# The last head pair's first patterns at the end of the far stretch, four projection chunks beside them, and V laid out and loaded by pairs of heads

## The chip, the cores and the metric

The kernel runs on one core of a Trainium2 chip: TensorE (PE) multiplies matrices, VectorE (DVE), ScalarE (ACT) and GpSimd (POOL) do the rest, and SyncE (SP) issues most DMAs. A core has 16 DMA engines. Each engine works through its own instructions in order, and an engine's DMAs stand in that same order: one that waits holds up what is behind it. The metric is the device time of one execution in microseconds, as the median over runs.

## The reference, cut to what matters

One layer of a hybrid encoder on x of 2048 tokens by 1024 features, in float32:

```python
y = rmsnorm(x, g) @ w_in
q, k, v = ...                     # 8 heads of 64; partial rotary on q and k
att = dilated_sliding_attention(q, k, v)
conv = conformer_conv(a, gate, ...)               # depthwise, 31 taps, layernorm, silu
h = x + concat([att, conv]) @ w_out
h = h + cross_attention(rmsnorm(h), rmsnorm(mem)) # 256 memory rows, 4 heads
h = h + square(relu(rmsnorm(h) @ w_up)) @ w_down  # 4096 wide
out = rmsnorm(h, g_final)

for window, d in ((128, 1), (512, 4), (2048, 16)):   # dilated_sliding_attention
    half = window // (2 * d)                         # tokens d apart, 64 to each side
    o, lse = banded_attention(strided(q, d), strided(k, d), strided(v, d), half)
o = sum(softmax(lses) * outs)                        # over the three patterns
```

So each head's attention has three patterns: the first (neighbours), the second (every 4th token) and the third (every 16th), and the three results are weighted by their softmax denominators and added.

## The kernel before, in words

Values are kept in two parts, a high part and the rest (`hi`/`lo`, `h`/`l`), and each product of two float32 matrices is three matmuls (`mm3`, lines 198 to 200). Tokens are worked on in four groups of 512 (p = 0 to 3).

*Start (to about 520 us).* Memory rows, x and the input projection. `lin_v` projects V and stores it as rows of `vtok` in DRAM: one row per token, 8 heads of 130 half floats (64 high, two ones, 64 low). Ahead of it `edges` writes 256 zero rows at each end of `vtok`, out of a tile `zrow` that takes a buffer of the tag `raw`, which the weight loads (`raw_k`, `raw_q` ...) use too.

*The far stretch (about 520 to 770 us).* `att(0, p2_)` works on group 0 and, since the third pattern mixes all tokens, on the third pattern of all four groups (`att_far`). It goes head by head through units of work: four far units, two of the second pattern, two of the first. A unit has three stages, one step apart: scores on PE, minimum (L773, DVE) and exponential (L774, ACT); transposes on PE and their split into `ph` and `pl` (L783, L784); the product with V (`opt`, L788 to L790). `att` yields twice per unit, and `weave` mixes these steps with another generator at a given rate: here the rest of the input projection (`rest`, tile `lin`). `pinned` and `after` hold the order on one engine to the order in which the code is traced; everything else a planner orders by a model of the times, and it draws instructions of later code forward where an engine would be idle in that model.

Far results go to DRAM (`oscr[pr][1]`, POOL's queue), so do the second pattern's (`oscr[pr][0]`). After a pair's last unit `then` starts `combine`: it loads both back (tile `ld`), takes the minimum (L904, L905), weights, sums into `cat`, transposes (`catT`, L940) and leaves the pair's rows `cath`, `catl`. For the last pair (`end`) the rows go straight into the tiles that the output projection reads, and DVE does what POOL does otherwise (`W`).

`load_v` fills three tiles for a pair of heads: `v3` for the far pattern (one DMA), `v2` for the second (eight) and `v1` for the first (five). Each has one buffer, so a load can start when the last product with the previous pair's V is done. In the far stretch all fourteen are issued behind a pair's last unit; in the later groups a pattern's loads are issued behind that pattern.

*After (from about 735 us).* `post(p)` does the output projection, cross attention and MLP of a group; beside it run attention (`att(p + 1)`) and convolution (`conv`, tile `cacc`) of the next. `resid_linear` does the output projection in chunks of 128 features, eight blocks (k) each, of which k = 2 and 3 in the order's last two places are the third and fourth head pair. For group 0 it starts with three chunks at once, so that four k, then two, then two are done for each:

```python
for ms in ((0, 1, 2), (3,), (4,), (5,), (6,), (7,)):
    for ks in (korder[0:4], korder[4:6], korder[6:8]) if len(ms) > 1 else (korder,):
```

The first six of these steps run beside the last steps of group 0's attention (`first`):

```python
weave(islice(pinned(main, "pe"), 6), (first, 2.4))
drain(first)
```

Weights come by `wpost`: a load into `raw` (two buffers), a cast on ACT (L189) and a subtraction on DVE (L190) into `whi` and `wlo`, two buffers in one pool (`wp`) and two in another (`wq`); `wq` takes memory that the far stretch's pool had, whose keys the last units still read. PSUM has eight banks; `banks` names which of them scores (`S`), transposes (`T`), products (`O`) and projections (`mm`) use in turn.

Of the kernel before, what the change touches and what calls it, by code (L numbers as in the profile page):

```python
# [12 lines left out]
F16 = mybir.dt.float16  # L13
# [34 lines left out]
def hybrid_layer(ctx, tc, A, out):  # L48
# [61 lines left out]
    vtok = dr.tile([256 + S + 256, VR], F16, name="vtok")  # L110
# [434 lines left out]
    def lin_v(g, ns):  # L545
# [18 lines left out]
        for t in range(4 * ns[0], 4 * ns[-1] + 4):  # L564
# [10 lines left out]
            s2 = st.rearrange("p h e -> p (h e)")  # L575
            gs = slice(g * 4 * VW, (g + 1) * 4 * VW)
            dma(vtok[256 + P * t:256 + P * (t + 1), gs], s2)
# [259 lines left out]
    def att_far(p2_, h, k, vt, q):  # L837
# [5 lines left out]
        def unit(rq, qh, ql):  # L843
# [40 lines left out]
    def combine(p, pr, o0):  # L884

        if p:
            yield
# [12 lines left out]
        end = p == 0 and pr == H // 2 - 1  # L900
# [6 lines left out]
        for i in range(2):  # L907
            W.tensor_tensor(e3[:, 1 + i], mm_, ld[:, i, :, :, HD + 1], op=ALU.subtract)
# [6 lines left out]
        for i in range(2):  # L915
            W.tensor_tensor(d3[:, 1 + i], e3[:, 1 + i], ld[:, i, :, :, HD], op=ALU.mult)
# [8 lines left out]
        for i in range(3):  # L925
            W.tensor_tensor(e3[:, i], e3[:, i], d2, op=ALU.mult)
        at = aq.tile([P, 4, 2, HD], F32, tag="cat", name=f"cat{p}{pr}")
        for i in range(3):
            src = ld[:, i - 1, :, :, 0:HD] if i else o0[:, :, :, 0:HD]
            W.tensor_tensor(src if i else at, src, e3[:, i].unsqueeze(3).to_broadcast([P, 4, 2, HD]), op=ALU.mult)  # L930
            if i:
                W.tensor_tensor(at, at, src, op=ALU.add)
# [15 lines left out]
    def att_units(p, far, then):  # L948
# [8 lines left out]
        def load_v(pr, pats):  # L957
            es = slice(pr * 2 * VW, (pr + 1) * 2 * VW)
            if 2 in pats and far:
                vt[2] = far.tile([P, 16, 2 * VW], F16, tag="v3", name=f"v3_{pr}")  # L960
                dma(vt[2], vtok[256:256 + S, es].rearrange("(i r) e -> i r e", r=16))
            if 0 in pats:
                vt[0] = aq.tile([P, 5, 2 * VW], F16, tag="v1", name=f"v1_{p}{pr}")
                for c in range(5):
                    t0 = 256 + 512 * p + P * c - 64
                    dma(vt[0][:, c], vtok[t0:t0 + P, es].rearrange("(i r) e -> r i e", r=16))
            if 1 in pats:
                vt[1] = aq.tile([P, 4, 2, 2 * VW], F16, tag="v2", name=f"v2_{p}{pr}")
                for c in range(2):
                    src = vtok[512 * (p + c):512 * (p + c) + 512, es].rearrange("(i a b) e -> b a i e", a=4, b=4)  # L970
                    for b in range(4):
                        dma(vt[1][:, b, c], src[b])

        def unit(pr, hh, pat, g, k, q_, opt, o0):
# [28 lines left out]
            for z in range(2):  # L1003
                blk = 2 * g + z
                for c in range(2):
                    vv = vt[1][:, blk, c] if pat else vt[0][:, blk + c]
# [21 lines left out]
        for pr in range(H // 2):  # L1028
            K = [load_keys(2 * pr + hh, p, hh) for hh in range(2)] if far else None
            o0 = aq.tile([P, 4, 2, ROW], F32, tag="o0", name=f"o0_{p}{pr}", bufs=2)  # L1030
            for hh in range(2):
                h = 2 * pr + hh
                if far:
# [3 lines left out]
                    yield from att_far(far, h, k, vt, q3)  # L1037
# [144 lines left out]
    def resid_linear(load, rhs, korder, resid, hs, ssum, key, y, name, steps=False):  # L1182
# [253 lines left out]
```

## Time and profile before

| | |
|---|---|
| runs, median (lowest to highest) | 2902.63 us (2901.68 to 2903.17) |
| profiled execution, its own time | 2896.44 us |
| its span | 2894.6 us |
| granted clock, mean | 0.992 |
| PE busy | 2826.2 us, 98% |
| DVE, ACT, POOL busy | 1860.5, 1167.0, 472.7 us |
| bytes moved, mean rate | 433.73 MB, 150 GB/s |
| V loads | 208 of 65 KB and 4 of 1040 KB |

The page gives busy time by engine, the chain of work that ended last and the costliest groups; other views give the same for a stretch, a list of who waited for whom, and the instructions in order of time. A line L57 is the helper that issues every DMA. PE's busy time counts a matmul as busy while it is in the pipeline, so rows of matmuls overlap; what counts is the idle time in brackets ahead of an instruction, with what ended it. A wait for several things is put down to the one that came last by the profile.

### The profile page before, as it was taken

To read this page: it belongs to the slowest core of one execution; us is meant where nothing else is said; L and a number is where in the kernel's file an instruction comes from. 1 tells how busy PE (TensorE), PEld (TensorE's weight loads), DVE (VectorE), ACT (ScalarE), POOL (GpSimd) and SP (SyncE) were. 2 spreads that over 40 slices of the span, in tenths; PEclk is the share of its full clock that TensorE was granted. 3 is DMA by queue.
4 is the path that set the end of the run, shared out by engine and by line. 5 is a ranking of instruction groups with operands and counts; after the bars stand their busy time and mean duration, and the time that the engine had idled before them with its cause. 6 is when DMAs were issued, how large, how long until landed. Compare 5 with 4: busy or idle time off the path is not lost.

```text
span 2894.6 us, 41429 instructions
## 1 busy us (share of the span) xinstructions
PE 2826.2 (98%) x15628; PEld 2377.7 (82%) x15628; DVE 1860.5 (64%) x3311; ACT 1167.0 (40%) x1988; POOL 472.7 (16%) x522
## 2 busy tenths in 40 slices
PE   8989999989899999999999999999999999999999
PEld 7878899878788888888888888888888888888888
DVE  5636536455689876566887756689877555544445
ACT  5623211466444343434543344445333433432233
POOL 1336431133002011200022012002111200000000
PEclk9999999999999999999999999999999999999999
DMA  8979854799834444545444546534543445233332
GB/s 259 295 157 228 200 146 134 178 232 237 219 98 127 142 132 126 170 145 164 124 124 128 146 116 192 175 100 121 143 127 115 139 131 175 90 93 100 97 95 73
DMA packets 606656, 433.73 MB, mean 150 GB/s; under 512 B 174886, under 2 KB 537434, under 8 KB 606457
## 3 DMA queue, kind: packets, MB, share of 16 engines
q1 hardware_dynamic: 566904, 408.81, 49.4%
q10 hardware_dynamic: 37952, 16.88, 2.3%
q0 software_dynamic: 1600, 5.41, 0.7%
q8 instruction: 123, 2.02, 0.3%
q14 instruction: 77, 0.62, 0.1%
HBM read 339.89 MB, written 91.11 MB: 149 GB/s over the span
## 4 chain that ended last, share of the span: by engine, by line
PE 84%; DVE 7%; DMA 4%; issue 2%; ACT 1%; SPq 1%; POOL 0%; POOLq 0%; DVEq 0%; ACTq 0%
PE dn L198 8%; PE dn L199 8%; PE dn L200 8%; PE up L198 8%; PE up L200 7%; PE up L199 7%; PE lin L198 4%; PE lin L200 3%; PE lin L199 3%; PE xs L198 2%; PE xs L200 2%; PE xs L199 2%; PE o L198 2%; PE o L199 2%; PE o L200 2%
## 5 line engine op out<-in xcount | busy, mean ns | idle before, releaser
L199 PE MATMUL dn<-hhl,whi_d 128*128 128x512 f32 (+1 forms) x1056 | 403.0, 384 | 1.4 <-DVE hhl L1310 1.4
L198 PE MATMUL up<-mh,whi_u 128*128 128x512 f32 x1024 | 402.6, 393 | 0.5 <-DVE rl L1307 0.5
L198 PE MATMUL dn<-hhh,whi_d 128*128 128x512 f32 (+1 forms) x1056 | 401.5, 391 | 1.1 <-ACT hhh L1309 1.1
L200 PE MATMUL dn<-hhh,wlo_d 128*128 128x512 f32 (+1 forms) x1056 | 402.1, 384 | 0.0
L199 PE MATMUL up<-ml,whi_u 128*128 128x512 f32 x1024 | 399.7, 390 | 1.6 <-DVE ml L1200 1.6
L200 PE MATMUL up<-mh,wlo_u 128*128 128x512 f32 x1024 | 399.8, 391 | 0.0
L215 DVE SCALAR_TENSOR_TENSOR cacc<-cu,cw,cacc 128x512 f32<-128x512 f32 x480 | 387.9, 808 | 5.5
L189 ACT CAST whi_d<-raw_d 128x1024 fp32r<-128x1024 f32 x128 | 134.6, 1052 | 424.8 <-PE up L199 380.0
L1325 DVE TENSOR_TENSOR h<-h,dn 128x512 f32<-128x512 f32 (+1 forms) x264 | 172.1, 666 | 161.8 <-PE dn L200 160.5
L189 ACT CAST whi_u<-raw_u 128x1024 fp32r<-128x1024 f32 x128 | 134.4, 1050 | 327.7 <-PE dn L199 299.6
L1307 DVE SCALAR_TENSOR_TENSOR rl<-up,ssumx 128x512 f32<-128x512 f32 x128 | 87.9, 690 | 260.6 <-PE up L200 256.4
L198 PEld LDWEIGHTS dn<-hhh,whi_d 128*128 128x128 f32 x1056 | 197.8, 188 | 40.7 <-DVE h L1325 3.5
L200 PEld LDWEIGHTS dn<-hhh,wlo_d 128*128 128x128 f32 x1056 | 198.4, 188 | 39.4
L199 PEld LDWEIGHTS dn<-hhl,whi_d 128*128 128x128 f32 x1056 | 198.8, 188 | 37.6 <-DVE hhl L1310 2.3
L199 PEld LDWEIGHTS up<-ml,whi_u 128*128 128x128 f32 x1024 | 192.5, 188 | 40.8 <-DVE ml L1200 3.0
L200 PEld LDWEIGHTS up<-mh,wlo_u 128*128 128x128 f32 x1024 | 192.3, 188 | 40.1
L198 PEld LDWEIGHTS up<-mh,whi_u 128*128 128x128 f32 x1024 | 192.4, 188 | 38.6 <-DVE rl L1307 0.9
L774 ACT ACTIVATE sm<-sm,o 128x256 f32<-128x256 f32 (+1 forms) x384 | 160.1, 465 | 121.8 <-DVE o L773 121.5
L190 DVE TENSOR_TENSOR wlo_u<-raw_u,whi_u 128x1024 fp32r<-128x1024 f32 x128 | 161.6, 1262 | 26.7 <-ACT whi_u L189 26.5
L190 DVE TENSOR_TENSOR wlo_d<-raw_d,whi_d 128x1024 fp32r<-128x1024 f32 x128 | 161.2, 1260 | 23.5 <-ACT whi_d L189 23.4
L773 DVE CUSTOM_DVE_ANT_0 sm<-s,mask 128x256 f32<-128x256 f32 (+1 forms) x384 | 128.3, 374 | 61.2 <-PE s L993 33.8
L176 POOL TENSOR_TENSOR nr<-st_v,mhalf 128x4 f32<-128x4 f32 (+1 forms) x13 | 13.4, 1031 | 845.7 <-DVE st_v L172 845.7
(402 smaller groups left out, 6341.1 us busy)
## 6 DMA issues: line engine op xcount, KB each, us to landing
raw_u<-in_w_up_dram SPq DMA_DIRECT2D x128, 512.0 KB
raw_d<-in_w_down_dram SPq DMA_DIRECT2D x128, 512.0 KB
raw_o<-in_w_out_dram SPq DMA_DIRECT2D x32, 512.0 KB
raw_a<-ascr SPq DMA_DIRECT2D x32, 512.0 KB
raw_b<-bscr SPq DMA_DIRECT2D x32, 512.0 KB
v<-vtok SPq DMA_DIRECT2D x208, 65.0 KB
k<-kscr SPq DMA_DIRECT2D x24, 512.0 KB
k<-kscr SPq DMA_DIRECT2D x8, 1152.0 KB
```

Of the source, the lines that this page charges most:

```text
L176: POOL.tensor_tensor(dst, v, mhalf.to_broadcast([P, v.shape[1]]), op=ALU.pow)
L189: ACT.copy(hi, raw)
L190: (lo_eng or DVE).tensor_tensor(lo, raw, f(hi), op=ALU.subtract)
L198: PE.matmul(o, lh, rh, start=first, stop=False)
L199: PE.matmul(o, lh, rl, start=False, stop=False)
L200: last["pe"] = PE.matmul(o, ll, rh, start=False, stop=end)
L215: DVE.scalar_tensor_tensor(acc, u[:, t:t + 512], cw[:, c, t:t + 1], acc, op0=ALU.mult, op1=ALU.add)
L773: last["dve"] = DVE.tensor_tensor_reduce(dst, so, mask[:, 256 * m:256 * m + nk], 1.0, 3e38, ALU.add, ALU.min, mn)
L774: last["act"] = ACT.activation(dst, dst, AF.Exp, bias=mn, scale=-1.0)
L1307: last["dve"] = DVE.scalar_tensor_tensor(r, pt, 0.0, rsb, op0=ALU.max, op1=ALU.mult)
L1325: last["dve"] = DVE.tensor_tensor(hs[m][:, sl], hs[m][:, sl], pt, op=ALU.add)
```

## The change

- `vtok` is laid out by pairs of heads: four blocks of 2560 rows with 260 half floats each. A V store writes two rows of 520 bytes per token where it wrote one of 1040. The zero rows are written out of 64 partitions in place of 16, still in two DMAs.
- `v3` and `v2` are read in longer runs: `v2` in two DMAs in place of eight (its tile now has the block inside), `v3` still in one, `v1` still in five. For group 1's first pair these loads go by POOL's queue.
- In the far stretch each pattern's V for the next pair is loaded when that pattern is done: `v3` behind the pair's last far unit (`done`), `v2` behind the second pattern, `v1` behind the first.
- For the last pair the first patterns of both heads come at the end, behind both heads' far and second patterns. The second pattern's store goes by SP, and the two loads of the partial sums (`load_sum`) are issued right behind it. For the other pairs of group 0 the minimum of `combine` comes two steps later. Small instructions of `combine` are merged, and one of its three multiplies goes to POOL for the last pair too.
- The output projection of group 0 starts with four chunks (`wide`), in cuts of four, two, one and one k; the fourth chunk has a bank of its own (`m3`, bank 4), and scores have one bank (3) in that time. The steps beside the end of the far stretch go by new rates. The convolution's first eight steps are pinned to PE's order.

```diff
-    vtok = dr.tile([256 + S + 256, VR], F16, name="vtok")
+    vtok = dr.tile([H // 2, 256 + S + 256, 2 * VW], F16, name="vtok")
...
-            dma(vtok[256 + P * t:256 + P * (t + 1), gs], s2)
+            dma(vtok[2 * g:2 * g + 2, 256 + P * t:256 + P * (t + 1)].rearrange("r t e -> t r e"),
+                st.rearrange("p (r h) e -> p r (h e)", r=2))
...
-        zrow = wp.tile([16, 1, VR], F16, tag="raw", name="zrow", bufs=2)
+        zrow = wp.tile([64, 1, VR], F16, tag="raw", name="zrow", bufs=2)
...
-        zb = zrow.to_broadcast([16, 16, VR])
+        zb = zrow.to_broadcast([64, 4, VR])
         for t0 in (0, 256 + S):
-            dma(vtok[t0:t0 + 256].rearrange("(q x) e -> q x e", q=16), zb)
+            dma(vtok[:, t0:t0 + 256].rearrange("r (q x) e -> q r (x e)", q=64), zb)
...
+            if rq == 3:
+                done()
...
-    def combine(p, pr, o0):
-
-        if p:
-            yield
+    def load_sum(p, pr):
         ld = aq.tile([P, 2, 4, 2, ROW], F32, tag="ld", name=f"ld{p}{pr}")
...
-        yield
-        yield
-        if p == 0:
-            for _ in range(2 if pr < 3 else 1):
+        return ld
+
+    lds = {}
+
+    def combine(p, pr, o0):
+
+        end = p == 0 and pr == H // 2 - 1
+        if end:
+            ld = lds[p, pr]
+        else:
+            if p:
+                yield
+            ld = load_sum(p, pr)
+            for _ in range(2 if p else 6):
                 yield
...
-        for i in range(2):
-            W.tensor_tensor(e3[:, 1 + i], mm_, ld[:, i, :, :, HD + 1], op=ALU.subtract)
+        W.tensor_tensor(e3[:, 1:3], mm_.unsqueeze(1).to_broadcast([P, 2, 4, 2]), ld[:, :, :, :, HD + 1],
+                        op=ALU.subtract)
...
-        for i in range(3):
-            src = ld[:, i - 1, :, :, 0:HD] if i else o0[:, :, :, 0:HD]
-            W.tensor_tensor(src if i else at, src, e3[:, i].unsqueeze(3).to_broadcast([P, 4, 2, HD]), op=ALU.mult)
-            if i:
-                W.tensor_tensor(at, at, src, op=ALU.add)
+        parts = [ld[:, i, :, :, 0:HD] for i in range(2)]
+        for i, x in ((2, parts[1]), (0, o0[:, :, :, 0:HD]), (1, parts[0])):
+            (POOL if i == 2 else W).tensor_tensor(x if i else at, x, e3[:, i].unsqueeze(3).to_broadcast([P, 4, 2, HD]),
+                                                  op=ALU.mult)
+        for x in parts:
+            W.tensor_tensor(at, at, x, op=ALU.add)
...
+            q = POOL if p == 1 and pr == 0 else None
...
-                vt[1] = aq.tile([P, 4, 2, 2 * VW], F16, tag="v2", name=f"v2_{p}{pr}")
+                vt[1] = aq.tile([P, 2, 4, 2 * VW], F16, tag="v2", name=f"v2_{p}{pr}")
                 for c in range(2):
-                    src = vtok[512 * (p + c):512 * (p + c) + 512, es].rearrange("(i a b) e -> b a i e", a=4, b=4)
-                    for b in range(4):
-                        dma(vt[1][:, b, c], src[b])
+                    dma(vt[1][:, c].rearrange("p b e -> p (b e)"),
+                        vtok[pr][512 * (p + c):512 * (p + c) + 512].rearrange("(i a b) e -> a i (b e)", a=4, b=4), q)
...
-                    os_.rearrange("p b h e -> p b (h e)"), POOL if far else nc.scalar)
+                    os_.rearrange("p b h e -> p b (h e)"),
+                    nc.scalar if not far else (nc.sync if pr == H // 2 - 1 else POOL))
+            if g and hh and pat and far and pr == H // 2 - 1:
+                lds[p, pr] = load_sum(p, pr)
...
-                    if not far:
-                        load_v(pr + 1, (pat,))
-                    elif not pat:
-                        load_v(pr + 1, (2, 1, 0))
+                    load_v(pr + 1, (pat,))
...
+                    if far and pr == H // 2 - 1 and pat == order[1]:
+                        tail.append((hh, k, qs))
+                        continue
...
+            for hh, k, qs in tail:
+                opt = []
+                yield from [unit(pr, hh, order[1], g, k, qs[order[1]], opt, o0) for g in range(2)]
...
-        for ms in ((0, 1, 2), (3,), (4,), (5,), (6,), (7,)):
+        for ms in ((0, 1, 2, 3) if wide else (0, 1, 2), () if wide else (3,), (4,), (5,), (6,), (7,)):
...
-            for ks in (korder[0:4], korder[4:6], korder[6:8]) if len(ms) > 1 else (korder,):
+            cuts = (0, 4, 6, 7, 8) if wide else (0, 4, 6, 8)
+            for ks in [korder[a:b] for a, b in zip(cuts, cuts[1:])] if len(ms) > 1 else (korder,):
...
-                        pts[m] = ps("mm", f"{name}{m}")
+                        pts[m] = ps("m3" if wide and m == 3 else "mm", f"{name}{m}")
...
-            weave(islice(pinned(main, "pe"), 6), (first, 2.4))
+            banks.update(S=(3,), m3=(4,))
+            main_ = pinned(main, "pe")
+            weave(islice(main_, 4), (first, 2))
+            weave(islice(main_, 8), (first, 0.5))
             drain(first)
-        sides = [(att(p + 1), 0.95), (conv(cv, p + 1), 0.6)] if p + 1 < NG else []
+        sides = []
+        if p + 1 < NG:
+            cg = conv(cv, p + 1)
+            if p == 0:
+                cg = chain(pinned(islice(cg, 8), "pe"), cg)
+            sides = [(att(p + 1), 0.95), (cg, 0.6)]
```

More of the change, by code (lines that the diff above doesn't have):

```diff
@@ L835, in far_q, with att_far @@
         return t, ql
-    def att_far(p2_, h, k, vt, q):
+    def att_far(p2_, h, k, vt, q, done):
         pr, hh = divmod(h, 2)
@@ L914, in combine @@
         W.tensor_tensor(d3[:, 0], e3[:, 0], o0[:, :, :, HD], op=ALU.mult)
-        for i in range(2):
-            W.tensor_tensor(d3[:, 1 + i], e3[:, 1 + i], ld[:, i, :, :, HD], op=ALU.mult)
+        W.tensor_tensor(d3[:, 1:3], e3[:, 1:3], ld[:, :, :, :, HD], op=ALU.mult)
         dn = sm_[:, 4]
@@ L924, in combine @@
         d2 = dn.rearrange("p (j h) -> p j h", h=2)
-        for i in range(3):
-            W.tensor_tensor(e3[:, i], e3[:, i], d2, op=ALU.mult)
+        W.tensor_tensor(e3, e3, d2.unsqueeze(1).to_broadcast([P, 3, 4, 2]), op=ALU.mult)
         at = aq.tile([P, 4, 2, HD], F32, tag="cat", name=f"cat{p}{pr}")
-        for i in range(3):
-            src = ld[:, i - 1, :, :, 0:HD] if i else o0[:, :, :, 0:HD]
-            W.tensor_tensor(src if i else at, src, e3[:, i].unsqueeze(3).to_broadcast([P, 4, 2, HD]), op=ALU.mult)
-            if i:
-                W.tensor_tensor(at, at, src, op=ALU.add)
+        parts = [ld[:, i, :, :, 0:HD] for i in range(2)]
[4 more added lines that the diff above has]
+            W.tensor_tensor(at, at, x, op=ALU.add)
         yield
@@ L1036, in att_units @@
                         keys = far_keys(far, h + 1)
-                    yield from att_far(far, h, k, vt, q3)
+                    yield from att_far(far, h, k, vt, q3, lambda: load_v(pr + 1, (2,)) if hh and pr < H // 2 - 1 else None)
                     qs = (q_, q_)
```

15 lines of the change are left out of this document (6 added, 9 removed).

## The prediction

> **What bounds the kernel now.** I read the page first, then busy time by stretch, then the waits of TensorE (PE), then the timeline around each wait. Columns of the second fence: stretch, its length, busy time (and instructions) of PE, PEld, DVE, ACT, POOL, granted clock, DMA share, GB/s.
>
> ```profile
> span 2894.6 us, 41429 instructions
> PE 2826.2 (98%) x15628; PEld 2377.7 (82%) x15628; DVE 1860.5 (64%) x3311; ACT 1167.0 (40%) x1988; POOL 472.7 (16%) x522
> ```
>
> ```profile
> 180.00:330.00 150.00, 140.75 (x629) 116.08 (x629) 83.63 (x104) 47.61 (x78) 80.91 (x70) 0.97 0.89 207
> 330.00:450.00 120.00, 120.00 (x715) 107.19 (x714) 55.27 (x81) 24.16 (x43) 35.39 (x48) 1.00 0.56 144
> 520.00:735.00 215.00, 196.93 (x1715) 173.01 (x1714) 118.46 (x492) 125.94 (x300) 57.91 (x77) 0.98 0.89 225
> 735.00:760.00 25.00, 22.90 (x170) 19.17 (x170) 13.16 (x35) 10.97 (x24) 3.66 (x4) 1.00 0.83 212
> 760.00:772.00 12.00, 4.05 (x25) 2.63 (x23) 8.78 (x28) 2.29 (x5) 2.22 (x2) 0.70 1.00 231
> 1500.00:2000.00 500.00, 499.78 (x2643) 414.54 (x2642) 359.35 (x601) 208.86 (x333) 59.84 (x69) 1.00 0.48 142
> ```
>
> PE sets the time. It does not wait where the V projection stores its rows (330 to 450) nor in the later groups (1500 to 2000), and its matrix work is unchanged: the change can only win PE's waits in three places. They are 9.25 us in 180 to 330, 18.07 in the far stretch (520 to 735) and 10.05 at its end (735 to 772), 37.4 in all, with the lowered clock behind them. What ended them (columns: start, duration, instruction, in brackets the wait and its releaser):
>
> ```profile
> 208.10 1.08 PE L332 MATMUL xt<-ident,xn 128*128 128x128 f32 x4 [7.45 <-DVE xv L337]
> 211.83 1.08 PE L332 MATMUL xt<-ident,xn 128*128 128x128 f32 x4 [1.79 <-DVE xv L337]
> 611.77 0.24 PE L790 MATMUL opt<-v,pl 128*128 128x65 f16 x1 [3.85 <-DVE pl L784]
> 663.57 0.20 PE L790 MATMUL opt<-v,pl 128*128 128x65 f16 x1 [2.32 <-DVE pl L784]
> 712.21 0.20 PE L790 MATMUL opt<-v,pl 128*128 128x65 f16 x1 [0.74 <-DVE pl L784]
> 737.67 0.20 PE L790 MATMUL opt<-v,pl 128*128 128x65 f16 x1 [1.36 <-DVE pl L784]
> 766.99 0.21 PE L788 MATMUL opt<-v,ph 128*128 128x65 f16 x1 [6.61 <-DMA v<-vtok]
> ```
>
> Behind the three `pl` waits from 611 to 713 stands, I read, the first minimum of `combine` (L904), which holds DVE in order until the partial sums `ld` are back (time waited, times, longest); behind the `xt` waits stands SP, held by the zero rows of `vtok`:
>
> ```profile
> DVE csm L904 <- DMA ld<-oscr: 6.8, 3, 3.2
> ```
>
> ```profile
> 182.88 12.24 DMA vtok<-zrow
> ```
>
> ```profile
> 195.18 1.70 SPq L57 DMA_DIRECT2D raw_k<-in_w_in_dram  x3
> 593.81 8.08 SPq L57 DMA_DIRECT2D v<-vtok  x8
> 604.08 0.56 SPq L57 DMA_DIRECT2D ld<-oscr  x1
> ```
>
> The weights `raw_k` take the zero rows' buffer, so SP stood still until 195.18, and with it the `xscr` stores that DVE and then PE wait for.
>
> **The change part by part.** *Zero rows.* Still two DMAs of 520 KB, but read from 64 partitions in place of 16. The first stretch below holds almost nothing but this transfer, the second mostly the far queries, which fill 64 partitions:
>
> ```profile
> 184.00:194.00 10.00, 10.00 (x50) 8.38 (x49) 5.40 (x7) 4.97 (x7) 4.70 (x4) 1.00 0.90 98
> 714.00:717.00 3.00, 3.00 (x30) 2.54 (x29) 1.70 (x7) 1.50 (x3) 1.43 (x7) 1.00 1.04 227
> ```
>
> 1.065 MB at 98 GB/s are 10.9 us, at 227 they are 4.7: SP goes on 6.2 us sooner, so does the chain behind it, and I take **6.0 us**. The ends are 0 (the rate does not depend on the partitions) and 11 (both waits, 9.24, and some clock). [...]
>
> *V stores and small edits: 0.* 32 stores write 256 rows of half the size in place of 128; PE does not wait in 330 to 450, and if that cover went, POOL, which refills their buffer, would be late. Each `combine` loses four tiny POOL instructions, off the path. The 12 V sets of the later groups go from 13 to 7 issues, under a PE that is busy 499.78 of 500.
>
> *V loads of the far stretch and the later minimum.* Per pair 14 issues become 8 (eight of `v2` to two), and they are spread: the far V when the last far unit is done, `v2` after the second pattern, `v1` after the first. So the two `ld` loads no longer have eight V issues (8.08) between them, and the minimum comes two steps (one unit) later. What goes: 3.85 + 2.32 + 0.74 = 6.9 us of PE waits, and of the clock (0.98 over 215 us) at most 4.3. What stays: the bytes. The stretch runs at a DMA share of 0.89, so some of it returns behind other loads; I take off 1 and count 1.6 of the clock: 6.9 - 1.0 + 1.6 = **7.5 us**. New on SP are stops: the far V waits there for the last far product, and behind it stand the next queries and keys. Ends: +11.2, and a loss priced as a rival below.
>
> *The end of the far stretch.* Before, both patterns of head 7 end last; then store, load and sum follow one another:
>
> ```profile
> 752.55 5.03 DMA oscr<-o
> 757.60 3.57 DMA ld<-oscr
> 761.19 0.17 DVE L904 TENSOR_TENSOR csm<-ld 128x8 f32<-128x8 f32 x1 [1.45 <-DMA ld<-oscr]
> 770.03 1.11 PE L940 MATMUL catT<-ident,cat 128*128 128x128 f32 x4 [0.19 <-DVE cat L932]
> 771.93 1.65 PE L198 MATMUL o<-cath,whi_o 128*128 128x512 f32 x3 [0.78 <-ACT cath L942]
> ```
>
> After, four units of the first pattern and sixteen blocks of projection run between store and sum, so store and load (8.6 us) are covered. Behind the last product PE has ten blocks before `catT`: four chunks by two k, then two more. A block is three matmuls that start 0.23 us apart,
>
> ```profile
> 758.87 0.39 PE L200 MATMUL o<-cath,wlo_o 128*128 128x512 f32 x1
> 759.10 0.39 PE L198 MATMUL o<-cath,whi_o 128*128 128x512 f32 x1
> ```
>
> that is 0.7 us, 7.0 together. The sum on DVE went from 761.19 to `catT` at 770.03, 8.8 us. Its parts in that stretch (busy time, mean of one):
>
> ```profile
> L215 DVE SCALAR_TENSOR_TENSOR cacc<-cu,cw,cacc 128x512 f32<-128x512 f32 x3 | 2.2, 747 | 0.0
> L930 DVE TENSOR_TENSOR ld<-ld,ce 128x512 f32<-128x512 f32 x2 | 1.3, 686 | 0.0
> L773 DVE CUSTOM_DVE_ANT_0 sm<-s,mask 128x256 f32<-128x256 f32 x2 | 0.8, 419 | 0.0
> L784 DVE TENSOR_TENSOR pl<-pt,ph 128x512 f16<-128x512 f32 x1 | 0.7, 676 | 0.0
> L926 DVE TENSOR_TENSOR ce<-ce,csm 128x8 f32<-128x8 f32 x3 | 0.3, 160 | 0.0
> ```
>
> 3.7 us (2.2 + 0.8 + 0.7) are convolution and group 1's probabilities, slipped in between. With the last copy out of PSUM ahead of it (0.7, as `pl`), four small instructions fewer (-0.4, at L926's 0.1 each) and one multiply given to POOL (-0.7) the sum takes 4.7 us alone and 8.4 with as much slipped in: against 7.0 PE waits 0 to 1.4 at `catT`, I take 1.0. Other waits that I leave: 1.36 (the row at 737.67, not touched); 1.0 for chunk 2's low weights, late already before
>
> ```profile
> 748.87 0.50 PE L200 MATMUL o<-cath,wlo_o 128*128 128x512 f32 x1 [0.74 <-DVE wlo_o L190]
> ```
>
> because their buffer lies under a far pool that closes late (an estimate, a little over this row); 1.0 for chunk 4, whose weight buffers come free only when chunk 0 is done, three blocks (2.1 us) ahead of its use; and 2.0 for the first V of group 1 (6.61 before), whose seven loads now go by POOL:
>
> ```profile
> oscr<-o POOLq DMA_DIRECT2D x20, 264.0 KB, 6.8
> 739.22 0.89 POOL L57 DMA_DIRECT2D oscr<-o  x1 [5.99 <-ACT o L868]
> ```
>
> Two issues (1.8) and a landing of 6.8 are 8.6 us against a cover of 7, up to five issues 11.3: 0 to 4. Left are 6.4 of 10.05 us; won are 3.7 and of the lost clock (0.70 over 12 us, at most 3.6) 2.3: **6.0 us**, between -4 (V, chunk 4 and the sum all late) and +12. With one bank for scores (`S`) a unit's scores wait for the minimum of the unit before; a chunk's 2.8 us lies between them, so 0.
>
> A rule that speaks against the multiply on POOL has a row here: the same subtraction took 1.81 us with a POOL cast beside it and 1.23 alone.
>
> ```profile
> 747.00 1.81 DVE L190 TENSOR_TENSOR wlo_o<-raw_o,whi_o 128x1024 fp32r<-128x1024 f32 x1
> 750.32 1.23 DVE L190 TENSOR_TENSOR wlo_o<-raw_o,whi_o 128x1024 fp32r<-128x1024 f32 x1 [0.81 <-ACT whi_o L189]
> ```
>
> [...]
>
> **Sum.** 6.0 + 7.5 + 6.0 = 19.5 us. The profiled execution took 2896.44 us (span and 1.8 around it); its forecast is 2876.9. The median of the runs, 2902.63, lies 6.2 us (0.2%) above it, so the runs should give 2883.1 us, 0.7% less. Under 0.2% (5.8 us) counts as no change: that is about what can be told.
>
> **The rivals.** *All waits go* (32 us: 11 + 10 + 11, 2871). For it: the three places hold 37.4 us and the clock. Against it: each step puts another wait close behind.
>
> *The DMA engines are the far stretch's second bound* (2895). For it: shares of 0.89, and 1.00 at its end, with the same bytes after; waits then change their names only, and the zero rows and a little more are won, 8 us. Against it: 231 GB/s at a share of 1.00 with small rows, and the far V's rows of 520 bytes become runs of 8320.
>
> *SP's new stops* (slower, 2914). Place: after the last far unit of pairs 0 to 2, the far V's load stands in SP until PE releases the tile, and the next queries behind it come late. Price: a query load on the chain,
>
> ```profile
> 662.48 7.76 DMA ql<-qfar
> ```
>
> three times 7.76 = 23.3 us, nothing won in the stretch: -6 - 6 + 23.3 = 11 us slower. It decides from 12 / 3 = 4 us per pair on. Against it: before, V's loads waited for PE in the same queue, later and with more behind them.
>
> **How the numbers follow.** Forecast 47% (2873 to 2892 alone), all waits 15%, DMA bound 24%, SP's stops 14%. The DMA case straddles the mark: 14% under 2896.8, 10% within 0.2%. Faster 47 + 15 + 14 = 76%, same 10%, slower 14%. The range 2868 to 2906 leaves out some 6% below and 13% above.
>
> **What would show it.** Zero rows: landing near 6 us in place of 12.24, `raw_k` near 189, the `xt` wait under 3. Far stretch: no wait of L904 over 1 us on DVE, PE busy over 203 of 215. End: no PE wait over 4 us between 735 and 772, the last k of chunks 0 to 3 in one run. Wrong it would be by a scores wait (L856, L857, L993) on `qfar` or `qscr` of several us in each pair, by a PE wait on `whi` or `wlo` of chunks 2 to 4, or by V of group 1 again ending a wait over 5 us.

## The result, and the profile after

The changed kernel takes 2910.39 us (median of 8 runs, 2907.17 to 2913.51) against 2902.75 for the kernel before (8 runs, 2897.47 to 2905.53): a ratio of 1.0026 with an interval of 1.0016 to 1.0036, 7.6 us slower. The forecast of 2883 is missed by 27 us and has the wrong sign. The profiled execution of after took 2912.79 us, 2.4 above its median; that of before lay 6.2 below its own, so the two traces differ by 16.4 us, of which about half is chance of the executions shown.

Busy time by stretch after (columns as in the prediction: stretch, length, PE, PEld, DVE, ACT, POOL, granted clock, DMA share, GB/s):

```profile
180.00:330.00 150.00, 145.49 (x648) 119.87 (x647) 87.36 (x106) 49.91 (x81) 84.36 (x73) 0.98 0.90 214
330.00:450.00 120.00, 120.00 (x715) 107.14 (x714) 50.91 (x76) 22.61 (x41) 32.63 (x46) 1.00 0.52 133
520.00:735.00 215.00, 194.48 (x1644) 170.46 (x1643) 113.58 (x476) 121.32 (x292) 56.25 (x66) 0.94 0.89 220
760.00:772.00 12.00, 9.03 (x41) 7.44 (x42) 5.81 (x18) 2.63 (x6) 0.00 (x0) 0.72 0.71 216
1500.00:2000.00 500.00, 497.37 (x2618) 412.16 (x2617) 354.60 (x591) 203.29 (x325) 56.92 (x57) 1.00 0.48 142
```

The first stretch won 4.7 us of PE time, as hoped. The far stretch, where 6 more were forecast, lost 2.5 (196.93 before), and the later groups, where PE had been busy 499.78 of 500, now wait 2.6. What PE waited for after, over the whole span (time, times, longest):

```profile
PE opt L789 <- DVE pl L783: 8.4, 10, 2.5
PE dn L198 <- DVE h L1338: 6.7, 3, 2.8
PE xt L332 <- DVE xv L337: 4.9, 4, 3.0
PE s L856 <- DMA ql<-qfar: 4.6, 2, 4.2
PE lin L198 <- DVE vst L574: 4.1, 1, 4.1
PE o L200 <- DVE wlo_o L190: 4.0, 1, 4.0
...
PE s L855 <- issue: 3.0, 1, 3.0
PE s L855 <- DMA qh<-qfar: 2.5, 1, 2.5
```

The old waits are smaller or gone (`xt` 9.6 to 4.9 us, no `v<-vtok` any more). Six others stand in their place. Where each costs is seen by the start of the same matmul in two traces (us, after less before): last V product -6.4, first far score +0.3, middle of the far stretch (score 192 of 768) -5.6, score 328 (the last ahead of head 7's) -0.2, score 384 (group 0's last) +11.3, first cross-attention matmul (`xs`, the far stretch is over) +6.6, last MLP matmul +16.8. So something takes 6.7 at the start of the far stretch, 17 in its second half and 10 in groups 1 to 3, while its first half gives back 6 and its end 5.

Not all of this is waiting. Behind the waits the granted clock falls: it was 0.51 from 509.6 to 516.5 us and 0.50 from 714.4 to 724.7. Over all runs, span times the missing share of the clock (an estimate from the two figures that each run lists) comes to 30 us after, 27 before and 19 in e2, the fast form below: of the 29 us between after and e2 some 11 are a lower clock and 18 are waits.

The first and the third of these losses have one neighbour. At the start of the far stretch (timeline of after: start, duration, instruction, in brackets the wait and its releaser):

```profile
492.07 1.16 SPq L57 DMA_DIRECT2D v<-vtok  x2
493.28 0.46 SPq L57 DMA_DIRECT2D lc<-cscr  x1
...
503.88 0.69 DVE L238 TENSOR_TENSOR lsum<-lc 128x512 f32<-128x512 f32 x1 [9.44 <-DMA lc<-cscr]
...
511.36 0.79 PE L198 MATMUL lin<-xh,whi_g 128*128 128x512 f32 x1 [4.10 <-DVE vst L574]
```

The pair of `v2` loads is issued just ahead of `lc`; DVE, in order, waits 9.44 us for `lc`, and PE waits for DVE. The same instruction before:

```profile
507.30 0.69 DVE L238 TENSOR_TENSOR lsum<-lc 128x512 f32<-128x512 f32 x1 [1.99 <-DMA lc<-cscr]
```

In group 1, after:

```profile
1093.09 1.14 SPq L57 DMA_DIRECT2D v<-vtok  x2
...
1093.90 0.33 ACTq L57 DMA_DIRECT2D oscr<-o  x1
...
1101.57 0.42 DVE L772 CUSTOM_DVE_ANT_0 sm<-s,mask 128x256 f32<-128x256 f32 x1 [5.79 <-DMA oscr<-o]
...
1105.95 0.50 PE L198 MATMUL dn<-hhh,whi_d 128*128 128x512 f32 x1 [2.84 <-DVE h L1338]
```

The same store before, beside eight short loads of the same bytes:

```profile
1085.20 5.76 SPq L57 DMA_DIRECT2D v<-vtok  x8
1086.01 0.33 ACTq L57 DMA_DIRECT2D oscr<-o  x1
1090.28 0.42 DVE L773 CUSTOM_DVE_ANT_0 sm<-s,mask 128x256 f32<-128x256 f32 x1 [2.39 <-DMA oscr<-o]
```

From issue to release of DVE the store took 4.3 us before and 7.7 after, and DVE's wait, harmless at 2.39 us, now reaches PE. Over the whole run:

```profile
DVE sm L773 <- DMA oscr<-o: 10.2, 4, 3.1
```

before, and after:

```profile
DVE sm L772 <- DMA oscr<-o: 22.9, 6, 5.8
```

The load itself is not slower: `v2` of this pair took 8.2 us before (1024 packets of 520 bytes) and 8.1 after (256 of 2080). In both its packets run about four at a time (3.9 and 3.6 on average), where 16 DMA engines are there. The second loss lies elsewhere in the main: 11.5 of the 17 us pass between scores 328 and 384, where PE waits for head 7's queries.

```profile
715.34 0.55 PE L855 MATMUL s<-k,qh 128*128 128x256 f32 x1 [2.97 <-issue]
720.13 0.58 PE L856 MATMUL s<-k,ql 128*128 128x256 f32 x1 [4.25 <-DMA ql<-qfar]
```

What belongs to the loads there, and what to the new end, the experiments show.

### The profile page after: what moved, and what is told of

Read it like the earlier page. It is cut to its first block, busy times and chain, and to the rows that moved or that the text cites. A ratio compares the mean times of both kernels' runs of the same rounds, so it can differ in the third digit from the quotient of the medians.

```text
span 2911.0 us, 41291 instructions
## 1 busy us (share of the span) xinstructions
PE 2839.2 (98%) x15628; PEld 2385.9 (82%) x15628; DVE 1857.8 (64%) x3306; ACT 1167.0 (40%) x1988; POOL 464.1 (16%) x469
## 4 chain that ended last, share of the span: by engine, by line
PE 82%; DVE 8%; DMA 6%; issue 2%; ACT 1%; SPq 1%; POOL 0%; POOLq 0%; DVEq 0%; ACTq 0%
PE dn L198 8%; PE dn L199 8%; PE dn L200 8%; PE up L198 7%; PE up L199 7%; PE up L200 7%; PE lin L198 4%; PE lin L200 4%; PE lin L199 4%; DVE cacc L215 2%; PE xs L198 2%; PE xs L200 2%; PE o L200 2%; PE o L198 2%; PE o L199 2%; PE xs L199 2%
```

## The experiments

Three theories were stated. Theory 1 (T1): a `v2` load goes over four DMA engines only, because the outer dimension of its source has size 4 (a), and two long ones hold up every transfer beside them that needs all sixteen. Theory 2 (T2): SP's new stops and the new places of the loads are to blame. Theory 3 (T3): the last pair, with one bank for scores. No trace names the engine of a packet: "four", "two" and "sixteen engines" stand below for an outer dimension of 4, of 2, and of 32 or 128, as theory 1 reads them; what was measured is how many packets run at a time. All results (median of 4 to 11 runs; the kernel before took 2902.3 to 2903.4 in the same sessions):

| kernel | us | ratio to before, interval |
|---|---|---|
| e1_v2_16eng | 2885.99 | 0.9947, 0.9933 to 0.9960 |
| e2_v2_contig | 2881.34 | 0.9925, 0.9913 to 0.9938 |
| e3_zero64_alone | 2897.61 | 0.9985, 0.9976 to 0.9994 |
| e4_v2_by_b | 2894.60 | 0.9970, 0.9960 to 0.9981 |
| e6_v2_two_engines | 2950.90 | 1.0164, 1.0151 to 1.0178 |
| e7_cut_late | 2890.84 | 0.9958, 0.9945 to 0.9970 |
| e8_old_end | 2883.03 | 0.9931, 0.9917 to 0.9944 |
| e9_old_load_order | 2885.11 | 0.9936, 0.9924 to 0.9949 |
| e10_before_v2_wide | 2902.16 | 0.9997, 0.9987 to 1.0006 |
| e11_v2_later | 2877.49 | 0.9914, 0.9899 to 0.9929 |
| e12_v2_later_dve_mult | 2879.11 | 0.9918, 0.9906 to 0.9931 |
| e13_end_alone | 2902.17 | 0.9996, 0.9987 to 1.0005 |
| e14_v2_16eng_8issues | 2887.08 | 0.9950, 0.9935 to 0.9964 |
| e15_v3_short_rows | 2884.12 | 0.9937, 0.9924 to 0.9951 |
| e16_head6_in_place | 2880.81 | 0.9929, 0.9915 to 0.9942 |

**What made it slow.** Four kernels came first: two ways to spread `v2` over sixteen engines, the zero rows alone, and the old eight loads in the new kernel.

```diff
 # e1, from after: each load cut by a, so that the outer dimension is 32
-  dma(vt[1][:, c]..., src)
+  for a in range(4):
+      dma(vt[1][32 * a:32 * a + 32, c].rearrange("p b e -> p (b e)"), src[a], q)
```

> The changed kernel with each v2 load of 260 KB cut into four of 65 KB by a (32 partitions each), so that the outer dimension on both sides is 32 in place of 4. T1 (a 260 KB load whose source has an outer dimension of 4 runs on few DMA engines, and what needs all engines queues behind it): the waits on lc at the lin/V boundary (lin 4.1 us), on qfar in the far stretch (10 us) and on oscr in groups 1 to 3 (h/dn 6.7 us) go, in all 20 to 30 us less than the changed kernel, 2880 to 2890 us; the 2080-byte packets of one load are in flight more than 8 at a time in place of 3 to 4. T2 (the new places of the V loads in SP's order hold the query loads): the same 2910 +-4, since places stay. T3 (the last pair's order and the single score bank): the same 2910 +-4.

```diff
 # e2, from after: two loads as before, over 128 rows that follow one another;
 # keys and mask of the second pattern take the same order
-  ....rearrange("(i a b) e -> a i (b e)", a=4, b=4)
+  ....rearrange("(i a b) e -> (i a) (b e)", a=4, b=4)
-  kv = k[:, blk:16:4, 0:64].rearrange("p r (c i) -> p c r i", c=2)
+  kv = k[:, blk:16:4, 0:64].rearrange("p r (c i) -> p c i r", c=2)
```

> The changed kernel with v2 still in two loads, but of 128 rows that lie one behind the other in DRAM (keys of the second pattern in the order token, so scores read their keys with a stride). T1: as the cut by a, 2880 to 2890, less some 2 us for fewer issues, plus whatever the strided keys cost PE (a score matmul of 128x256 now starts 0.12 us after the one before; if it takes twice that, some 30 us more over 256 of them by two). T2 and T3: 2910 or more.

```diff
 # e4, from after: eight loads of 520-byte rows, as before
+  src = ....rearrange("(i a b) e -> b a i e", a=4, b=4)
+  for b in range(4):
+      dma(vt[1][:, c, b], src[b], q)
```

> The changed kernel with v2 loaded by b in eight DMAs of 65 KB with 520-byte rows, as before the change, in the new layout; still an outer dimension of 4. T1 in the form that one long transfer on few engines does the harm (short ones let others in between, and SP issues them apart): 2885 to 2895. T1 in the form that only the number of engines counts: 2910 +-4, as the bytes per engine are the same. T2 (places in SP's order): 2910 or more, as SP is held longer.

Both wide forms are 24 and 29 us faster than the changed kernel, and faster than the kernel before, with every place of the loads and the last pair as changed. Theory 1 holds as far as the packets show it; theories 2 and 3 fall as the main cause. A pair's packets run 5 to 8 at a time on average in e1 (more than 8 were expected) and 9 to 13 in e2, in place of 3.6, and take 3.8 to 5.6 and 2.5 to 3.6 us in place of about 8. In e2 the waits for `h` and `vst` are not in the list; the waits for `qfar`, which were to go as well, are still 5.0 us in e1 and 4.9 in e2, and DVE's wait for the store in e2 is down to

```profile
DVE sm L772 <- DMA oscr<-o: 3.3, 3, 1.6
```

If few engines do it, two engines must be worse:

```diff
 # e6, from after: two loads of two a's each, outer dimension 2
+  for a in (0, 2):
+      dma(vt[1][32 * a:32 * a + 64, c].rearrange("p b e -> p (b e)"), src[a:a + 2], q)
```

> The changed kernel with each v2 load cut in two by pairs of a (outer size 2 in place of 4, twice as many issues, same bytes, same packets of 2080 bytes). Theory 1 (a long transfer on few DMA engines holds up what lies beside it): the packets of one load run at most about 4 at a time in the trace, a pair's 256 packets take longer than the 8.1 us of the changed kernel (10 to 16), the waits for oscr and qfar grow, and the time is 5 to 25 us above the changed kernel's 2910. Rival (it is the size of the packets or the number of issues, not the engines): within 4 us of 2910, or nearer to 2900 because there are more issues.

2950.9 us, 40 above the changed kernel, beyond the expected 5 to 25. A pair's packets run 1.9 at a time and take 13 to 14 us. Its waits, over the whole run:

```profile
PE dn L198 <- DVE h L1339: 13.1, 5, 5.2
PE lin L198 <- DVE vst L574: 7.8, 1, 7.8
PE s L855 <- issue: 7.3, 2, 6.9
```

These are the waits of the changed kernel, doubled. Where the loss lies was asked by cutting the loads in groups 1 to 3 alone:

```diff
 # e7, from after
+  if p == 0:
+      dma(vt[1][:, c]..., src, q)
+  for a in range(4 if p else 0):
+      dma(vt[1][32 * a:32 * a + 32, c]..., src[a], q)
```

> The changed kernel with the v2 loads cut by a (outer size 32) in groups 1 to 3 alone, and as changed in group 0. Theory 1 puts 10.9 us of loss in groups 1 to 3 and the rest into the start of the far stretch and its second half: the waits of PE for h behind oscr go, the shift from the end of the far stretch to the end of the kernel falls from +10.9 to between -5 and 0, and the time is 2895 to 2899. Rival (the later groups lose what the far stretch hands on, not by their own loads): 2905 to 2910.

2890.8: by the medians 19.5 of the 24.4 us that e1 wins come from the loads of groups 1 to 3, more than the 11 to 15 expected, and 4.9 from group 0. The traces say less: of the 24.4 us between that of after and e7's, 14.2 lie behind `xs`, 5.1 between score 328 and `xs`, and 5.1 ahead of score 328, where both kernels load alike, so that part is chance of the executions shown. Are few engines enough by themselves? The kernel before has had them all along:

```diff
 # e10, from before: the same eight issues, each over 128 rows (keys and mask as in e2)
-  src = ....rearrange("(i a b) e -> b a i e", a=4, b=4)
+  src = ....rearrange("(m b) e -> b m e", b=4)
```

> The kernel before with its v2 loads in the same eight issues of 65 KB and the same rows of 520 bytes, but each over 128 rows in one run of the outer dimension (the key order of pattern 2 is changed to fit) in place of 4 by 32. Theory 1, carried over to the kernel before: its own eight loads also sit on about four engines (8.2 us each pair), so it gains too: DVE's waits for oscr in groups 1 to 3 (7.1 us in three) go and with them the PE waits for h, and part of the far stretch: 4 to 11 us faster than before. Rival (eight short loads do no harm, since others slip in between): within 3 us of before.

```diff
 # e14, from e2: eight issues of 520-byte rows, sixteen engines
+  src = ....rearrange("(m b) e -> b m e", b=4)
+  for b in range(4):
+      dma(vt[1][:, c, b], src[b], q)
```

> The kernel with v2 in 128 rows that follow one another (2881.3), but with each pair's v2 in eight issues of 65 KB (rows of 520 bytes) in place of two of 260 KB. With the runs so far it fills a table of two by two: four engines and two issues 2910.4, four engines and eight issues 2894.6, sixteen engines and two issues 2881.3. If the harm is that of few engines alone: 2881 to 2884. If eight issues cost by themselves (SP's time, 8 us a pair in the far stretch): 2886 to 2893.

e10 changes nothing (the rival holds): DVE's wait for the store fell there from 10.2 to 1.0 us, but before the change PE did not wait behind it, and another wait grew: DVE's for `ld`, from 6.8 to 17.0 us. e14 completes a table:

| `v2` of a pair | four engines | sixteen engines |
|---|---|---|
| eight issues of 65 KB | 2894.6 (e4) | 2887.1 (e14) |
| two issues of 260 KB | 2910.4 (after) | 2881.3 (e2) |

On sixteen engines fewer issues win 5.8 us; on four they lose 15.8. The packet records of the store beside the load say why. Each store of `oscr` has 128 packets of 2112 bytes, eight for each of 16 engines if they are spread evenly. Counted from the first of them, in group 1:

| kernel | on time | late packets | one load's share of an engine, an estimate (packets by theory 1 x mean ns of one) |
|---|---|---|---|
| before | 96 by 0.84 us | 32, from 1.44 to 2.62 us | 32 x 31 = 1.0 us |
| after | 96 by 0.93 us | 32, from 3.92 to 5.71 us | 32 x 114 = 3.6 us |
| e6 | 112 by 0.86 us | 16, from 3.28 to 4.93 us | 32 x 94 = 3.0 us |
| e2 | 127 by 1.29 us | 1, at 1.37 us | 8 x 127 = 1.0 us |

Late is exactly the share that four engines of sixteen would have (32 of 128), or two (16). The same split (96, 96 and 112 on time) stands in nine of the eleven stores that have a `v2` load beside them, in each of the first three kernels, and in none of e2's. And in the row of each kernel the share is late by about what one load, by that estimate, puts on each of its engines: the store's packets there seem to wait until the load's whole share has passed. In the changed kernel six of the nine stores agree (first late packet at 2.96 to 3.92 us, a share of 3.2 to 3.8); in the other three, where the load's packets began with the store's own, it came at 1.98 to 2.55 us, so a whole share is not always waited for. The counts of late packets agree with four engines and with two; which engines they were stands in no trace, and how long an engine stays with one load was not shown.

**What the three terms are worth.** The zero rows alone:

```diff
 # e3, from before
-  zrow = wp.tile([16, 1, VR], ...);  zb = zrow.to_broadcast([16, 16, VR])
+  zrow = wp.tile([64, 1, VR], ...);  zb = zrow.to_broadcast([64, 4, VR])
```

> The kernel before with the zero rows written from 64 partitions and nothing else. Theory: landing near 6 us in place of 12.24, raw_k near 189, the xt waits 4.5 us in place of 9.2; 5 to 6 us faster than before, 2897. Rival (the changed kernel's early gain has another cause, and the bytes set the write's time): no change, 2902.7 +-2.

4.65 us faster than the 2902.26 of its session. The order of the loads and the later minimum, and the long rows of `v3`, each taken back from e2:

```diff
 # e9, from e2
-  load_v(pr + 1, (pat,))
+  if not far: load_v(pr + 1, (pat,))
+  elif not pat: load_v(pr + 1, (2, 1, 0))
-  for _ in range(2 if p else 6):
+  for _ in range(2 if p else 4):
```

> The kernel with v2 in 128 rows that follow one another (2881.3), with a pair's V loads of the far stretch issued all behind its last unit and the minimum two steps sooner, as before. By my prediction's term of 7.5 it is slower by 5 to 9 us (2886 to 2890), with DVE waiting for ld again in three places. Rival (SP's new stops cost as much as the spread wins, as the waits for qfar that are left say): 2877 to 2883, with the qfar waits between 650 and 735 gone.

```diff
 # e15, from e2: a padded tile keeps the rows at 520 bytes
-  vt[2] = far.tile([P, 16, 2 * VW], ...)
+  vt[2] = far.tile([P, 16, 2 * VW + 2], ...)
```

> The kernel with v2 in 128 rows that follow one another (2881.3), with the far pattern's V read in rows of 520 bytes in place of runs of 8320 (its tile padded by two half floats a row). The zero rows (4.7), the spread of the loads (3.8) and the end (1.7) leave some 11 us of its gain over the kernel before without a name. If the long runs of v3 carry part of them: 3 to 8 us slower. Rival (the same bytes, so the same time): within 2 us of 2881.

3.8 us for the order, 2.8 for the rows (between the two times expected of e15); each is a difference of two medians, good to some 3 us, and neither is clear of nothing. In e9 the old wait is back,

```profile
PE opt L789 <- DVE pl L783: 13.1, 12, 5.6
```

and the wait for `qfar` falls from 4.9 to 0.4, while one of 4.4 for `qscr` comes, so both expectations had a half right. The end of the far stretch, taken back from e2 and put alone into the kernel before:

```diff
 # e8, from e2; e13 is its reverse, from before
-  if far and pr == H // 2 - 1 and pat == order[1]: tail.append(...); continue
-  lds[p, pr] = load_sum(p, pr)                 # behind an early store by SP
-  banks.update(S=(3,), m3=(4,));  weave(islice(main_, 4), (first, 2));  weave(islice(main_, 8), (first, 0.5))
+  weave(islice(pinned(main, "pe"), 6), (first, 2.4))
   # three chunks at the start, all multiplies on DVE, group 1's V on SP
```

> The kernel with v2 in 128 rows that follow one another (2881.3), with the end of the far stretch as it was before (three chunks, both patterns of the last head last, store and load of the partial sums behind them, multiply on DVE, group 1's first V on SP). By my prediction's term of 6.0 it is slower by that: 2885 to 2890, with the V wait of 6 us and the store-load-sum sequence back between 735 and 772. Rival (the end's gain was only handed from one wait to the next): within 3 us of 2881.

> The kernel before with the end of the far stretch alone as changed (last pair's first patterns last, early store and load of its partial sums, four chunks, merged small instructions, group 1's first V by POOL); V's layout, its loads and their times, the zero rows and the minimum as before. My prediction's term: 6.0 us faster, between -4 and +12. Rival, from the run that put the old end back (2883.0 against 2881.3): 0 to 2 us faster, because waits in the stretch before take its place.

It is worth 1.7 us on top of the rest and 0.4 alone, in place of 6.0; neither can be told from nothing, and the rivals hold. With the old end (e8) PE waits where it did before:

```profile
PE opt L787 <- DMA v<-vtok: 7.4, 1, 7.4
...
PE catT L943 <- DVE cat L935: 4.0, 1, 4.0
```

but not for `qfar`. With the new end alone (e13) these are gone and two others came:

```profile
721.08 0.55 PE L856 MATMUL s<-k,qh 128*128 128x256 f32 x1 [3.79 <-DMA qh<-qfar]
...
764.19 0.58 PE L1001 MATMUL s<-k,ql 128*128 128x256 f32 x1 [7.61 <-DMA ql<-qscr]
```

The first pattern of head 6, moved to the end, used to run while head 7's far queries came in. The starts of matmuls say the same (us between two of them; PE has the same projection and V products to do in each column, in either form):

| | score 328 to 384 | score 384 to `xs` |
|---|---|---|
| old end: before, e8 | 34.7, 32.9 | 57.9, 62.0 |
| new end: e13, e2, after | 41.2, 43.3, 46.2 | 56.1, 52.7, 53.2 |

What the new end wins behind score 384 it has lost ahead of it, with `v2` on four engines or on sixteen. So 6.5 (e13) to 8.6 (e2) of the 11.5 us that the changed kernel loses there are the new end's, and 3 to 5 are left for the loads. The 5.4 us between scores 192 and 328 stay open: 67.3 us before, 72.7 after, but 71.3 in e1 and 64.5 in e2. And group 1, which no longer waits for V, waits for its queries, which before were late by little, behind the V wait:

```profile
768.21 0.58 PE L993 MATMUL s<-k,ql 128*128 128x256 f32 x1 [0.16 <-DMA ql<-qscr]
```

**Versions of the fast form.** Three more changes were tried on e2:

```diff
 # e11, from e2: in the far stretch v2 is loaded with v1, behind the last unit
+  elif not pat: load_v(pr + 1, (1, 0))
 # e12, from e11: the third multiply back on DVE
-  (POOL if i == 2 else W).tensor_tensor(...)
+  W.tensor_tensor(...)
 # e16, from e11: head 6's first pattern in its place, only head 7's at the end
-  if far and pr == H // 2 - 1 and pat == order[1]:
+  if far and pr == H // 2 - 1 and hh and pat == order[1]:
```

> The kernel with v2 in 128 rows that follow one another (2881.3), with v2 of the far stretch loaded behind the pair's last unit, just ahead of v1, in place of behind the second pattern. In that kernel's trace SP stands 8.22 us at a v2 load from 676.15 on, ahead of the next queries, and PE waits 4.9 us for ql behind qfar. If SP's stop is the cause: the stop and the wait go, 2 to 5 us faster (2876 to 2879). Rival (the qfar loads are late for the bytes ahead of them): within 2 us of 2881, the wait stays or moves.

> As e11_v2_later, with the last pair's third multiply back from POOL on DVE. In the trace with it on POOL that multiply took 1.56 us on POOL and the one beside it on DVE 1.54 in place of 0.69. If the two exclude each other: DVE's three multiplies take 2.07 in place of 2.23, and the time is within 2 us of e11. Rival (POOL's multiply saves 0.7 as my prediction counted): 0.7 slower, which these rounds can't tell from nothing; the trace's rows decide.

> As e11_v2_later (2877.5), with the first pattern of head 6 back in its place and only head 7's at the end. Theory: head 6's two units were the cover of head 7's queries, and moving them made the wait for ql behind qfar (3.58 at 701.67); back in place the wait is under 1 us and the end has two units (5 to 6 us) less to cover the store and load of the sums (8.6 us), so it loses there: 2874 to 2880, with the loss moved from 700 to 740-770. Rival (the wait is that of the bytes): the wait stays at 3 us or more.

e11 is the fastest kernel of the study, 2877.5 us, 0.86% under the kernel before (its lead of 3.8 over e2 is within what the intervals leave open). SP's long stop goes, first e2, then e11:

```profile
676.15 8.22 SPq L57 DMA_DIRECT2D v<-vtok  x2
```

```profile
686.64 1.96 SPq L57 DMA_DIRECT2D v<-vtok  x2
...
701.67 0.58 PE L856 MATMUL s<-k,ql 128*128 128x256 f32 x1 [3.58 <-DMA ql<-qfar]
```

yet the wait for `ql` went only from 4.85 to 3.58 us, so the stop was not its main cause; the rival that the wait stays is the better half. In e16 that wait is gone, which confirms that head 6's units were its cover, and the end pays for them (timeline of e16):

```profile
758.77 1.12 PE L946 MATMUL catT<-ident,cat 128*128 128x128 f32 x4 [7.66 <-DVE cat L938]
```

The median is 3.3 us above that of e11, with ranges that overlap: the two units are needed in both places. Of the multiply the rows decide. After, POOL and DVE beside each other; and in e12 DVE alone:

```profile
777.77 1.56 POOL L935 TENSOR_TENSOR ld<-ld,ce 128x512 f32<-128x512 f32 x1 [1.18 <-issue]
778.35 1.54 DVE L935 TENSOR_TENSOR ld<-ld,ce 128x512 f32<-128x512 f32 x1
```

```profile
757.39 0.69 DVE L935 TENSOR_TENSOR ld<-ld,ce 128x512 f32<-128x512 f32 x1
758.00 0.69 DVE L935 TENSOR_TENSOR cat<-o,ce 128x512 f32<-128x512 f32 x1
```

With POOL's help the multiplies take DVE 0.69 + 1.54 = 2.23 us, without it 3 x 0.69 = 2.07. e11 and e12 can't be told apart by time.

## Why the prediction was wrong

**The step that failed** is "eight of `v2` to two", in *V loads of the far stretch and the later minimum* and again in "The 12 V sets of the later groups go from 13 to 7 issues, under a PE that is busy 499.78 of 500", counted there at 0. It priced an issue by SP's time and the load by its bytes ("What stays: the bytes"), and asked neither how many DMA engines a load uses nor what stands beside it on those. The trace of before could have told: 1024 packets of 520 bytes in 8.2 us, four at a time, and a store of which a quarter came late. Merged, each load puts, by the author's estimate, 3.6 us of packets on each of its four engines in place of 1.0 (32 of 114 ns, 32 of 31). That cost 15.8 us against eight issues on the same four engines (after against e4) and 29.1 against the same two issues on sixteen (after against e2). Most of it, 14 us by the traces and 19.5 by the medians of e7, fell in the groups where the term was 0. The 3.9 us of clock that the sum counted as won (1.6 and 2.3) did not come either: the far stretch was granted 0.94 in place of 0.98.

**Zero rows: right.** -6.0 forecast, -4.65 alone. After, the rows land in 7.22 us in place of 12.24 (near 6 was said), SP reaches `raw_k` at 188.58 (195.18 before; "near 189" was said), and the `xt` waits are 3.02 and 1.49:

```profile
180.55 1.34 SPq L57 DMA_DIRECT2D vtok<-zrow  x2
...
188.58 2.13 SPq L57 DMA_DIRECT2D raw_k<-in_w_in_dram  x3
...
201.97 0.67 PE L332 MATMUL xt<-ident,xn 128*128 128x128 f32 x4 [3.02 <-DVE xv L337]
204.99 1.09 PE L332 MATMUL xt<-ident,xn 128*128 128x128 f32 x4 [1.49 <-DVE xv L337]
```

A zero-row packet took 154 ns from 64 partitions and 300 from 16 (medians of 512 in the traces of after and before).

**V loads and the later minimum: right on sixteen engines as far as can be told, its form fatal on four.** With sixteen engines the parts measure 3.8 (order and minimum), 5.8 (two issues for eight) and 2.8 (long rows of `v3`), 12.4 us where 7.5 were forecast, each good to some 3 us; the mechanism is seen in the wait for `pl`, 13.1 us with the old order (e9) and 6.0 with the new (e2). With four, two issues for eight lose 15.8. "No wait of L904 over 1 us" and "PE busy over 203 of 215" both failed: DVE waited 3.8 once, and PE was busy 194.48.

**The end: priced in its own window.** PE's waits of over 0.9 us between 735 and 785 are two after:

```profile
744.42 0.63 PE L779 MATMUL pt<-ident,sm 128*128 128x128 f32 x4 [1.45 <-DVE ctl L949]
...
762.97 0.80 PE L200 MATMUL o<-cath,wlo_o 128*128 128x512 f32 x1 [4.01 <-DVE wlo_o L190]
```

For low weights 1.0 was taken for each of two chunks; they take 4.01 once, just over the 4 that was given as a sign. V of group 1 is gone, and from score 384 to `xs` the changed kernel wins 4.7 us, near the 6.0. But e8 and e13 show 1.7 and 0.4, and the 6.5 to 8.6 us lost between scores 328 and 384 say why: the units that cover the end had been cover for head 7's queries, and what came behind the V wait was late too. The term asked what would cover the moved store and not what the moved units had covered. Saving 0.7 by the multiply on POOL was the smaller error: DVE's multiply beside POOL's took 1.54 us in place of 0.69, so by the rows of after and e12 it cost 0.16. The prediction's own rows of the subtraction, 1.81 us beside a POOL cast and 1.23 alone, pointed that way.

**V stores: 0, right.** PE is busy 120.00 of 120 where they stand, and e1 and e2 win with the stores as changed.

**The rivals.** *SP's new stops* had the sign, and its 2914 lies near 2910 by luck: with the same stops and sixteen engines the kernel is 16 to 21 us faster than before, and PE waited for queries at the second heads of pairs (668, 715 and 720 us), not at the first ones, where the rival put it. *All waits go* fell with 8.4 us for `pl` and 4.9 for `xt` left. *The DMA engines are the far stretch's second bound* fell too: in e2 the stretch runs at a share of 0.98 and PE is busier than before.

```profile
520.00:735.00 215.00, 199.43 (x1745) 175.15 (x1744) 123.28 (x503) 130.05 (x310) 56.80 (x68) 0.97 0.98 237
```

The sum of the measured terms, -4.7 - 12.4 - 1.7 + 29.1 = +10.3 us against +7.6, is no proof that they are complete: the step from four engines to sixteen with eight issues, 7.5 us in the new kernel (e4 to e14) and 0.4 in the old (e10), is not in it, so the terms depend on what stands beside them. The forecast itself, 2883.1, is met by the sixteen-engine forms (2877.5 to 2887.1), but with parts of other sizes than forecast, so in part by luck. Left open are how long a store's packets stand behind a load's, which was read from counts and not varied by itself, and the 5.4 us between scores 192 and 328.

## What to carry to other kernels

Before loads are merged, look at how many of their packets run at a time: the packets of these loads ran 2 at a time with an outer dimension of 2, 4 with 4, and 5 to 13 with 32 or 128, and beside the longer load with 4 the last quarter of a store's packets landed from 3.92 us on in place of 1.44. Put a large dimension outermost first (32 and 128 did here), even by changing the order of keys, and merge then. A wait that costs nothing in the profile of before (2.39 us of DVE behind a store) is the first thing to check when transfers beside it change; and when work is moved to cover something, ask what it covered where it stood.

## What was not expected of the hardware

Two DMAs with the same bytes and the same duration (8.1 and 8.2 us) differed by 3.1 us in what they cost a neighbour: the last quarter of a 264 KB store landed at 5.71 us in place of 2.62, beside packets of 114 ns in place of 31; that it stood behind them on four engines is the author's reading of the counts. With an outer dimension of 2 the pair of loads takes 13 to 14 us and its packets run 1.9 at a time, though twice as many issues carry it: the counts show no sign that the two halves spread over engines of their own.
